# Sums of squares of x read from V's buffers, and V's last weights split before q and k are finished

## The chip, the core and the metric

The kernel runs on one core of one Trainium2 chip. The core has TensorE (matrix products), VectorE (DVE), ScalarE (ACT), GpSimd (POOL) and SyncE (SP), which issues nearly all transfers here. The metric is the device time of one launch in microseconds (us); lower is better.

## The reference, cut to what matters

The layer takes 512 tokens of width 1024. Of it, this change touches the root mean square norm at the start and the projections behind it.

```python
def rmsnorm(x, g):
    xf = x.astype(jnp.float32)
    y = xf * lax.rsqrt(jnp.mean(xf * xf, axis=-1, keepdims=True) + RMS_EPS)
    return (y * g.astype(jnp.float32)).astype(x.dtype)
...
        h = rmsnorm(x, g_mix[i])
        proj = h @ w_in[i]
        q_sb, k_sb, v_sb, z_sb, q_mb, k_mb, v_mb, z_mb = jnp.split(proj, split_at, axis=-1)
```

Eight stick-breaking heads (sb) and eight block heads (mb, with a slope times the distance of key and query, and a causal mask) follow. Their normed and gated outputs go through w_out, are added to x, and a second gated projection of p is added after another norm. All is float32.

## The kernel before, in words

Every float32 product is made of three TensorE products: an operand is split into a high part (cast on ScalarE, `part_hi`) and a low part (the difference, on VectorE, `part_lo`), and `mul3` multiplies high by high, high by low and low by high. x comes in twice: transposed (`xT`, four loads into `xt`), to be scaled by the gains and split into `hT` (`hT_hi`, `hT_lo`, eight slices k); and by tokens (`xs`, four loads of 512 KB), whose only use is the sum of squares of each token (`sq_x`, on ScalarE, with an accumulator). The norm's factor r (`find_r`: one VectorE step, one power on GpSimd) is not applied to `hT` but to the results of the projections: as a column of four numbers to V, and spread over a whole tile (`spread_r`: four TensorE transposes, one ScalarE copy) to q and k.

Weights are loaded in units of 512 KB into three buffers (tag `raw`), in the order q0, k0, the four V units, q1, k1 and on. Here the V units are called Vu0 to Vu3. A unit is split by two casts and two differences of 128x512, which `split_unit` puts into a queue; each `pop_w` issues the next cast and the difference of the cast before. The second difference of a unit frees its raw buffer and issues the load of the unit three further on. So Vu1's load follows q0's split, Vu2's follows k0's, and Vu3's follows Vu0's.

TensorE works through an order written by hand: warming products, the products of p with w_ple (`ple`), q0 and k0 (24 products each), V for token tiles 0 and 1 (48 products; k = 0, 1 use Vu0; 2, 3 use Vu1; 4, 5 use Vu2; 6, 7 use Vu3), the scores of head 0, and then a stream in which heads and projections alternate to the end. The four transposes of `spread_r` stand between k0's step 6 and step 7. The scores of head 0 need `end_q0` and `end_k0`: each takes the projection out of its bank times r (`scaled`, one VectorE product into the single buffer `ev`), then casts and differences: for q four casts of 64x512 on ScalarE, two differences on VectorE, and two zero fills on GpSimd; for k two casts and two differences.

Inside the section `start` the instructions of ScalarE and VectorE keep the order in which the program writes them. SyncE and (before) GpSimd are ordered by the planner; so are the instructions of ScalarE and VectorE written after the section, and the planner can put those between the ones inside it. The buffers of tag A and C, used later by the heads, hold `xt` first and `xs` second, so that load t of x waits until `hT_lo` has read chunk t of `xt`. The tag v has two buffers of 8 KB a partition for V's two halves, unused until V is taken out. `pl_d` is a DRAM tile into which the eight results of `ple` are parked by 256 KB stores. `rel` is the table of distances with the mask; `front_mb` scales it on ScalarE before each block head, by 4 for the first and by 0.5 for each later one.

Of the kernel before, what the change touches and what calls it, by code (L numbers as in the profile page):

```python
# [8 lines left out]
F32 = mybir.dt.float32  # L9
F32R = mybir.dt.float32r  # L10
BF16 = mybir.dt.bfloat16
AF = mybir.ActivationFunctionType
OP = mybir.AluOpType
ET = mybir.EngineType

P = 128
S = 512
DM = 1024
KT = DM // P
HD = 64  # L20
NH = 8
NPAIR = 8
DPLE = 256
NT = S // P
EPS = 1e-6
QKS = 0.125
NEG = -1e30
# [7 lines left out]
def layer(ctx, tc, x, xT, pT, w_qkz, w_v, gcols, g_final, w_out, w_ple, w_gate, out):  # L35
# [12 lines left out]
    nc = tc.nc  # L48
# [7 lines left out]
    at = ctx.enter_context(tc.tile_pool(name="at", bufs=2))  # L56
    dram = ctx.enter_context(tc.tile_pool(name="dram", bufs=1, space=bass.MemoryType.DRAM))
    pp = ctx.enter_context(tc.tile_pool(name="pp", bufs=1, space=bass.MemoryType.PSUM))
    ctx.enter_context(tc.manual_schedule(engines={ET.PE}))
    start = tc.manual_schedule(engines={ET.Activation, ET.DVE})  # L60
    start.__enter__()

    pl_d = dram.tile([NT, P, DM], F32, name="pl_d")
# [16 lines left out]
    def part_hi(hi, src, scale=None):  # L80
        if scale is None:
            nc.scalar.copy(hi, src)  # L82
        else:
            nc.scalar.activation(hi, src, AF.Copy, scale=scale)

    def part_lo(hi, lo, src, scale=None):
        if scale is None:
            nc.vector.tensor_sub(lo, src, hi.bitcast(F32))  # L88
        else:
            nc.vector.scalar_tensor_tensor(lo, src, scale, hi.bitcast(F32), op0=OP.mult, op1=OP.subtract)  # L90
# [11 lines left out]
    fq, wq, late = deque(), deque(), []  # L102
    pend = []

    def pop_w():
        if wq:
            hi, lo = wq.popleft()
            hi()
            if pend:
                pend.pop(0)()  # L110
            pend.append(lo)
        elif pend:
            pend.pop(0)()
# [43 lines left out]
    def load(tile_, src):  # L157
        nc.sync.dma_start(tile_, src)  # L158

    def load_unit():  # L160
        if n_load[0] == len(UNITS):
            return
        kind, a, u = key = UNITS[n_load[0]]
        n_load[0] += 1
        r = raws[key] = raw.tile([P, DM], F32, name="raw")
        if kind == "v":
            load(r, w_v[a, u])
        elif kind == "V":
            load(r.rearrange("p (g c) -> p g c", g=2),
                 w_v[:2, u // 2, :, u % 2 * S:(u % 2 + 1) * S].rearrange("g p c -> p g c"))  # L170
        elif kind == "o":
            half, n = a
            row = (4 * half + 2 * u) * P
            load(r.rearrange("p (k c) -> p k c", k=2),
                 w_out[row:row + 2 * P, n * S:(n + 1) * S].rearrange("(k p) c -> p k c", p=P))
        elif kind == "g":
            load(r, w_gate[a * P:(a + 1) * P, :])
        else:
            load(r, w_qkz[12 * (a // 4) + BASE[kind] + a % 4])

    def gate_tiles(k):

        if k < 2:
            if k == 0:
                wg["big"] = big.tile([P, 2, 2, DM], F32R, name="wg01", tag="hTl")
            w = wg["big"][:, k]
        elif k == 2:
            w = at.tile([P, 2, DM], F32R, name="wg2", tag="v")
        elif k == 3:
            w = wu.tile([P, 2, DM], F32R, name="wg3", tag="wu")  # L190
        else:
            tags = {4: ("QH0", "QH1", "K0", "K1"), 5: ("QH0", "QH1", "K0", "K1"), 6: ("QL0", "QL1", "QL0", "QL1"),
                    7: ("y0", "y1", "y2", "y3")}[k]
            w = [(yp if g[0] == "y" else at).tile([P, S], F32R, name=f"wg{k}{i}", tag=g)
                 for i, g in enumerate(tags)]
            return [(w[n], w[2 + n]) for n in range(2)]
        return [(w[:, 0, n * S:(n + 1) * S], w[:, 1, n * S:(n + 1) * S]) for n in range(2)]

    def split_unit():

        if n_split[0] == len(UNITS):
            return
        kind, a, u = key = UNITS[n_split[0]]
        n_split[0] += 1
        parts = []
        scale = gc[:, 2 * KT + a:2 * KT + a + 1] if kind == "g" else None

        def hi_(n):
            if not parts:
                if kind == "g":  # L210
                    wg[a] = gate_tiles(a)
                    parts.extend(wg[a])
                else:
                    w = W_[key] = wu.tile([P, 2, DM], F32R, name="wu")
                    parts.extend((w[:, 0, n * S:(n + 1) * S], w[:, 1, n * S:(n + 1) * S]) for n in range(2))
            part_hi(parts[n][0], raws[key][:, n * S:(n + 1) * S], scale)

        def lo_(n):
            part_lo(*parts[n], raws[key][:, n * S:(n + 1) * S], scale)
            if n:  # L220
                whole.add(key)
                load_unit()

        wq.extend((lambda n=n: hi_(n), lambda n=n: lo_(n)) for n in range(2))
        if n_split[0] < len(UNITS) and UNITS[n_split[0]][0] == "g":
            split_unit()
# [37 lines left out]
    load_unit()  # L264
    load_xt(3)
    load_unit()
    xs = [at.tile([P, DM], F32, name=f"xs{t}", tag="A" if t < 2 else "C") for t in range(NT)]

    def load_xs(t):
        load(xs[t], x[t * P:(t + 1) * P, :])  # L270

    for t in range(NT):
        load_xs(t)
# [10 lines left out]
    own = cst.tile([P, S], F32, name="own")  # L284
    nc.gpsimd.memset(own, 0.0)
    nc.gpsimd.affine_select(out=own, in_=own, compare_op=OP.not_equal, fill=1.0, base=S - P,
                            pattern=[[-1, S]], channel_multiplier=1)
    rel = at.tile([P, S], F32, name="rel", bufs=1)
    nc.gpsimd.iota(rel, pattern=[[1, S]], base=-384, channel_multiplier=-1,
                   allow_small_or_imprecise_dtypes=True)  # L290
    nc.gpsimd.affine_select(out=rel, in_=rel, compare_op=OP.is_ge, fill=NEG, base=384,
                            pattern=[[-1, S]], channel_multiplier=1)


# [209 lines left out]
    ss4, r4 = (cst.tile([P, NT], F32, name=n) for n in ("ss4", "r4"))  # L504

    def sq_x(t):
        junk = at.tile([P, DM], BF16, name="junk", tag="o")
        nc.scalar.activation(junk, xs[t], AF.Square, accum_out=ss4[:, t:t + 1])

    def find_r():  # L510

# [57 lines left out]
    for t in range(NT):  # L569
        sq_x(t)  # L570
# [6 lines left out]
    spread_r()  # L577
    F0(1)
    end_q0, end_k0 = first
    end_q0()  # L580
    split_unit()
    for _ in range(3):
        pop_w()
    end_k0()
    for t in range(NT):
        for n in range(2):
            load(pl_d[t, :, n * S:(n + 1) * S], pls[t, n])
    F0(8)
    pop_w()
    pop_w()  # L590

    start.__exit__(None, None, None)


    def scores(h):
        pr, e = divmod(h, 2)
        (Qh, Ql), k_ = Q[pr], K[pr][e]
        sc = pp.tile([P, 3 * S], F32, name="sc")
        for i in (3, 2, 0, 1):
            n = P * (i + 1)  # L600
            o = sc[:, OFF[i]:OFF[i] + n]
            q = slice(i * P, (i + 1) * P)
            mm(o, Qh[e][:, q], k_[:, :n], True, False)
            mm(o, Ql[e][:, q], k_[:, :n], False, True)
        return sc

    def rows(i):
        return OFF[i], OFF[i] + P * (i + 1)
# [34 lines left out]
        ])  # L643

    def front_mb(h):
        nc.scalar.activation(rel, rel, AF.Copy, scale=0.5 if h > NH else 0.5 / QKS)
        sc = scores(h)
        s = at.tile([P, WID], F32, name="A")
        w = W[h] = at.tile([P, WID], F32, name="C")
        m, nm, l, rl = (sm.tile([P, NT], F32, name=n) for n in ("m", "nm", "l", "rl"))  # L650

        def top(i):
            a, b = rows(i)
            nc.vector.tensor_tensor_reduce(out=s[:, a:b], in0=sc[:, a:b], in1=rel[:, S - (b - a):], scale=1.0,
                                           scalar=-3e38, op0=OP.add, op1=OP.max, accum_out=m[:, i:i + 1])

        def neg(c):
            nc.vector.tensor_scalar_mul(nm[:, c], m[:, c], -QKS)  # L658

        def exp(i):  # L660
            a, b = rows(i)
            nc.scalar.activation(w[:, a:b], s[:, a:b], AF.Exp, scale=QKS, bias=nm[:, i:i + 1],  # L662
                                 accum_out=l[:, i:i + 1])

        def inv(c):
            nc.vector.reciprocal(rl[:, c], l[:, c])

        def norm(i):
            a, b = rows(i)
            nc.vector.tensor_scalar_mul(w[:, a:b], w[:, a:b], rl[:, i:i + 1])  # L670

        hi, lo = slice(2, 4), slice(0, 2)
        fq.extend([
            lambda: top(3),
            lambda: (top(2), neg(hi)),
            lambda: (exp(3), exp(2), top(0), top(1), neg(lo)),
            lambda: (exp(0), exp(1)),
            lambda: (inv(hi), norm(3), norm(2)),
            lambda: (inv(lo), norm(0), norm(1)),
        ])  # L680
# [249 lines left out]
    t = NT - 1  # L930
# [75 lines left out]
```

## Time and profile before

| | us |
|---|---|
| median of 3 runs | 358.45 |
| lowest and highest | 357.63, 358.76 |
| the profiled execution, device time | 358.52 |
| its span, first to last instruction | 356.7 |
| TensorE busy | 345.5 (97%) |
| VectorE busy | 274.1 (77%) |
| ScalarE busy | 222.8 (62%) |
| GpSimd busy | 20.1 (6%) |

The device time of the profiled execution is 1.8 us above its span. The granted TensorE clock was 0.995 of full speed over the span. A busy share of TensorE counts pipelined products, whose recorded durations overlap; the distance from one start to the next is what a product costs.

### The profile page before, as it was taken

The page shows a single profiled execution, that of the slowest core. Times are in us where ns is not written, and L with a number is a line of the kernel's source. Part 1 is how long each engine was busy: PE and PEld are TensorE (multiplying, and loading weights), DVE is VectorE, ACT ScalarE, POOL GpSimd, SP SyncE. Part 2 cuts the span into 40 slices and gives each one's busy share as a digit, 9 for nine tenths or more (in the row PEclk, how much of TensorE's full clock was granted, in tenths as well). Part 3 has the DMA queues.
Part 4 walks back from the last instruction along what each step waited for, and adds up shares of the span by engine and source line. Part 5 has one row for each costly group of instructions (what it writes and reads, how often), then busy time and mean ns, then how long its engine had stood idle before and what let it go on. Part 6 is the DMA issues. An engine that isn't in the chain of part 4 may idle for free.

```text
span 356.7 us, 5077 instructions
## 1 busy us (share of the span) xinstructions
PE 345.5 (97%) x1808; PEld 292.1 (82%) x1808; DVE 274.1 (77%) x560; ACT 222.8 (62%) x421; POOL 20.1 (6%) x43
## 2 busy tenths in 40 slices
PE   8998899999999999999999999999999999999991
PEld 6786788888888888899888899888888888888891
DVE  4746779979898987988789888889799987244454
ACT  4887567664867464775596787598676662343341
POOL 6001000000000000000000100000000010010011
PEclk9999999999999999999999999999999999999998
DMA  6988907111131113112311302311811650022221
GB/s 214 379 291 272 311 9 232 62 61 59 59 119 60 59 62 130 56 64 104 122 59 61 118 3 59 119 59 30 326 59 63 212 200 0 7 100 71 90 89 59
DMA packets 14953, 40.18 MB, mean 113 GB/s; under 512 B 1616, under 2 KB 1872, under 8 KB 14928
## 3 DMA queue, kind: packets, MB, share of 16 engines
q1 hardware_dynamic: 14784, 39.60, 32.5%
q8 instruction: 14, 0.23, 0.3%
q10 hardware_dynamic: 144, 0.26, 0.2%
q14 instruction: 11, 0.09, 0.1%
HBM read 35.66 MB, written 4.19 MB: 112 GB/s over the span
## 4 chain that ended last, share of the span: by engine, by line
PE 84%; DMA 6%; issue 3%; DVE 2%; SPq 2%; ACT 1%; POOL 0%; POOLq 0%; ACTq 0%; DVEq 0%
PE pj L70 62%; PE sc L70 8%; PE tp L73 6%; PE av L70 6%; DMA raw<-in_w_qkz_dram 4%; DMA raw<-in_w_v_dram 2%; SPq L158 2%; PE tp L70 1%; DVE wu L88 1%; ACT wu L82 1%; DVE hTl L90 0%; DVE K L330 0%; POOL r L99 0%; POOLq L1002 0%; DVE ot L927 0%
## 5 line engine op out<-in xcount | busy, mean ns | idle before, releaser
L70 PE MATMUL pj<-hTh,wu 128*128 128x512 f32 x384 | 133.7, 400 | 0.0
L70 PEld LDWEIGHTS pj<-hTh,wu 128*128 128x128 f32 x384 | 72.2, 188 | 13.5 <-DVE wu L88 0.4
L70 PE MATMUL pj<-hTl,wu 128*128 128x512 f32 x192 | 75.1, 391 | 0.0
L82 ACT CAST wu<-raw 128x512 fp32r<-128x512 f32 x80 | 46.6, 617 | 23.1 <-PE pj L70 21.3
L88 DVE TENSOR_TENSOR wu<-raw,wu 128x512 fp32r<-128x512 f32 x80 | 52.7, 684 | 3.8 <-ACT wu L82 3.4
L70 PE MATMUL pj<-wg,h 128*128 128x512 f32 (+1 forms) x216 | 46.2, 371 | 0.0
L70 PEld LDWEIGHTS pj<-wg,h 128*128 128x128 f32 x216 | 36.9, 188 | 6.9
L70 PEld LDWEIGHTS pj<-hTl,wu 128*128 128x128 f32 x192 | 36.2, 189 | 5.2
L70 PE MATMUL pj<-wu,hTh 128*128 128x256 f32 (+1 forms) x160 | 34.2, 308 | 0.0
L82 ACT CAST ph<-tp 128x512 fp32r<-128x512 f32 (+1 forms) x48 | 24.5, 511 | 14.7 <-PE tp L73 14.4
L88 DVE TENSOR_TENSOR plo<-tp,ph 128x512 fp32r<-128x512 f32 (+1 forms) x48 | 28.5, 594 | 4.6 <-ACT ph L82 4.4
L70 PE MATMUL pj<-wu,yh 128*128 128x512 f32 x96 | 30.9, 402 | 0.0
L626 DVE TENSOR_TENSOR_SCAN inc<-A,own 128x512 f32<-128x512 f32 (+3 forms) x32 | 24.6, 809 | 5.6 <-ACT A L621 5.5
L70 PEld LDWEIGHTS pj<-wu,hTh 128*128 128x128 f32 x160 | 25.8, 191 | 1.3
L73 PE MATMUL tp<-idf,C 128*128 128x128 f32 x160 | 25.2, 272 | 0.0
L73 PEld LDWEIGHTS tp<-idf,C 128*128 128x128 f32 x160 | 20.3, 140 | 5.6
L70 PE MATMUL pj<-wu,hTl 128*128 128x256 f32 (+1 forms) x80 | 24.3, 304 | 0.0
L305 DVE TENSOR_TENSOR ev<-pj,rx 128x512 f32<-128x512 f32 x24 | 16.5, 686 | 6.3 <-PE pj L70 6.1
L70 PE MATMUL sc<-K,QH 128*128 128x512 f32 (+1 forms) x64 | 19.8, 322 | 0.0
L70 PE MATMUL av<-ph,v 128*128 128x512 f32 (+1 forms) x64 | 19.7, 309 | 0.0
L662 ACT ACTIVATE C<-A,nm 128x512 f32<-128x512 f32 (+3 forms) x32 | 17.8, 557 | 2.4 <-DVE nm L658 2.3
L70 PE MATMUL av<-plo,v 128*128 128x512 f32 (+1 forms) x64 | 19.1, 324 | 0.0
(135 smaller groups left out, 565.5 us busy)
## 6 DMA issues: line engine op xcount, KB each, us to landing
raw<-in_w_qkz_dram SPq DMA_DIRECT2D x24, 512.0 KB, 3.6
raw<-in_w_v_dram SPq DMA_DIRECT2D x8, 512.0 KB, 3.6
raw<-in_w_out_dram SPq DMA_DIRECT2D x8, 512.0 KB, 4.0
raw<-in_w_gate_dram SPq DMA_DIRECT2D x8, 512.0 KB, 3.6
xt<-in_xT_dram SPq DMA_DIRECT2D x4, 512.0 KB, 8.4
xs<-in_x_dram SPq DMA_DIRECT2D x4, 512.0 KB, 4.9
pl_d<-pt SPq DMA_DIRECT2D x8, 256.0 KB, 5.7
x<-in_x_dram SPq DMA_DIRECT2D x4, 512.0 KB, 6.5
```

The source lines that it names most:

```text
L70: nc.tensor.matmul(ps, lhsT=lhsT, rhs=rhs, start=start, stop=stop)
L73: nc.tensor.transpose(ps, src, idf)
L82: nc.scalar.copy(hi, src)
L88: nc.vector.tensor_sub(lo, src, hi.bitcast(F32))
L158: nc.sync.dma_start(tile_, src)
L305: nc.vector.tensor_mul(t, ps, rx["all"])
L626: nc.vector.tensor_tensor_scan(inc[:, c:c + b - a][:, ::-1], keep[:, a:b][:, ::-1], own[:, S - (b - a):][:, ::-1], 0.0, op0=OP.mult, op1=O ...
L662: nc.scalar.activation(w[:, a:b], s[:, a:b], AF.Exp, scale=QKS, bias=nm[:, i:i + 1], accum_out=l[:, i:i + 1])
```

## The change

Four edits. x by tokens is loaded into two tiles with V's tag, two token tiles each; token tiles 0 and 2 are squared on ScalarE as before, 1 and 3 on VectorE in place, with an accumulator. Behind `spread_r` the order on ScalarE and VectorE is: three pops (Vu2, and the first cast of Vu3), `end_q0`, the rest of Vu3, `end_k0`, and q1 only after that; before it was `end_q0`, three pops, `end_k0`, with the rest of Vu3 behind. GpSimd too keeps program order in the section, and `rel` is built at the section's end rather than at the kernel's start. `rel` is built with the factor 4 in it, so that the first block head scales nothing.

```diff
-    start = tc.manual_schedule(engines={ET.Activation, ET.DVE})
+    start = tc.manual_schedule(engines={ET.Activation, ET.DVE, ET.Pool})
...
-    xs = [at.tile([P, DM], F32, name=f"xs{t}", tag="A" if t < 2 else "C") for t in range(NT)]
+    xs = [at.tile([P, 2, DM], F32, name=f"xs{t}", tag="v") for t in range(2)]
...
-        load(xs[t], x[t * P:(t + 1) * P, :])
+        load(xs[t // 2][:, t % 2], x[t * P:(t + 1) * P, :])
...
-    rel = at.tile([P, S], F32, name="rel", bufs=1)
-    nc.gpsimd.iota(rel, pattern=[[1, S]], base=-384, channel_multiplier=-1,
-                   allow_small_or_imprecise_dtypes=True)
-    nc.gpsimd.affine_select(out=rel, in_=rel, compare_op=OP.is_ge, fill=NEG, base=384,
-                            pattern=[[-1, S]], channel_multiplier=1)
...
-        junk = at.tile([P, DM], BF16, name="junk", tag="o")
-        nc.scalar.activation(junk, xs[t], AF.Square, accum_out=ss4[:, t:t + 1])
+        x_ = xs[t // 2][:, t % 2]
+        if t % 2:
+            nc.vector.tensor_tensor_reduce(out=x_, in0=x_, in1=x_, scale=1.0, scalar=0.0, op0=OP.mult, op1=OP.add,
+                                           accum_out=ss4[:, t:t + 1])
+        else:
+            junk = at.tile([P, DM], BF16, name="junk", tag="o")
+            nc.scalar.activation(junk, x_, AF.Square, accum_out=ss4[:, t:t + 1])
...
     end_q0, end_k0 = first
-    end_q0()
-    split_unit()
     for _ in range(3):
         pop_w()
+    end_q0()
+    while wq or pend:
+        pop_w()
     end_k0()
+    split_unit()
     for t in range(NT):
         for n in range(2):
             load(pl_d[t, :, n * S:(n + 1) * S], pls[t, n])
...
+    rel = at.tile([P, S], F32, name="rel", bufs=1)
+    step = int(0.5 / QKS)
+    nc.gpsimd.iota(rel, pattern=[[step, S]], base=-384 * step, channel_multiplier=-step,
+                   allow_small_or_imprecise_dtypes=True)
+    nc.gpsimd.affine_select(out=rel, in_=rel, compare_op=OP.is_ge, fill=NEG, base=384,
+                            pattern=[[-1, S]], channel_multiplier=1)
     start.__exit__(None, None, None)
...
-        nc.scalar.activation(rel, rel, AF.Copy, scale=0.5 if h > NH else 0.5 / QKS)
+        if h > NH:
+            nc.scalar.activation(rel, rel, AF.Copy, scale=0.5)
```

## Rows read from the trace of the kernel before

**Rows 1.** The page: 40 slices of 8.9 us, TensorE's busy tenths and transfer rate.

```profile
PE   8998899999999999999999999999999999999991
...
GB/s 214 379 291 272 311 9 232 62 61 59 59 119 60 59 62 130 56 64 104 122 59 61 118 3 59 119 59 30 326 59 63 212 200 0 7 100 71 90 89 59
```

**Rows 2.** Waits of TensorE, 16 to 44 us: total, times, longest (us).

```profile
PE av L70 <- DVE wu L88: 1.4, 2, 1.1
PE tp L73 <- POOL r L99: 0.7, 1, 0.7
```

**Rows 3.** Timeline of TensorE: start, duration, instruction, count, idle before and releaser.

```profile
26.68 0.39 PE L70 MATMUL pj<-hTh,wu 128*128 128x512 f32 x1
27.73 0.65 PE L73 MATMUL tp<-idf,r 128*128 128x128 f32 x4 [0.67 <-POOL r L99]
...
34.13 0.39 PE L70 MATMUL tp<-wu,hTl 128*128 128x512 f32 x1
...
34.84 0.50 PE L70 MATMUL av<-wu,hTh 128*128 128x512 f32 x1 [0.32 <-ACT wu L82]
...
35.65 0.50 PE L70 MATMUL av<-wu,hTh 128*128 128x512 f32 x1 [0.31 <-DVE wu L88]
...
38.26 0.43 PE L70 MATMUL av<-wu,hTh 128*128 128x512 f32 x1
...
39.78 0.50 PE L70 MATMUL av<-wu,hTh 128*128 128x512 f32 x1 [1.09 <-DVE wu L88]
...
42.41 0.39 PE L70 MATMUL sc<-K,QH 128*128 128x512 f32 x1
```

**Rows 4.** Timeline of ScalarE, VectorE and GpSimd, 15 to 40 us.

```profile
15.05 0.62 ACT L646 ACTIVATE rel<-rel 128x512 f32<-128x512 f32 x1
...
20.70 1.06 ACT L508 ACTIVATE junk<-xs 128x1024 bf16<-128x1024 f32 x1
...
21.16 1.28 DVE L88 TENSOR_TENSOR wu<-raw,wu 128x512 fp32r<-128x512 f32 x2
...
26.39 0.17 DVE L98 TENSOR_SCALAR rs_t<-ss 128x4 f32<-128x4 f32 x1 [3.94 <-ACT junk L508]
...
26.65 1.03 POOL L99 TENSOR_TENSOR r<-rs_t,mhalf 128x4 f32<-128x4 f32 x1 [20.31 <-DVE rs_t L98]
27.15 1.29 DVE L88 TENSOR_TENSOR wu<-raw,wu 128x512 fp32r<-128x512 f32 x2 [0.59 <-ACT wu L82]
...
36.23 1.27 ACT L329 CAST K<-ev 64x512 fp32r<-64x512 f32 x2
...
36.99 1.40 DVE L330 TENSOR_TENSOR K<-ev,K 64x512 fp32r<-64x512 f32 x2
...
38.43 1.89 DVE L88 TENSOR_TENSOR wu<-raw,wu 128x512 fp32r<-128x512 f32 x3
```

**Rows 5.** Timeline of SyncE's issues, 5 to 29 us.

```profile
5.89 0.58 SPq L158 DMA_DIRECT2D raw<-in_w_qkz_dram  x1
...
7.26 0.96 SPq L158 DMA_DIRECT2D raw<-in_w_qkz_dram  x1
14.39 6.61 SPq L158 DMA_DIRECT2D xs<-in_x_dram  x4
21.05 1.79 SPq L158 DMA_DIRECT2D raw<-in_w_v_dram  x3
...
28.48 0.37 SPq L158 DMA_DIRECT2D raw<-in_w_v_dram  x1
```

**Rows 6.** Issue to landing by tile: raw (6 to 9 us), raw (22 to 30).

```profile
DMA to landing us min/median/max: 9.6/10.1/10.7
...
DMA to landing us min/median/max: 3.6/5.4/7.2
```

**Rows 7.** VectorE by form: reduction of two inputs; busy us, mean ns, idle before.

```profile
L654 DVE CUSTOM_DVE_ANT_0 A<-sc,rel 128x512 f32<-128x512 f32 x8 | 5.5, 683 | 0.6 <-PE sc L70 0.6
...
L654 DVE CUSTOM_DVE_ANT_0 A<-sc,rel 128x128 f32<-128x128 f32 x8 | 2.3, 283 | 0.0
```

## Prediction

> **What bounds the kernel now.** I read the 40 slices first. TensorE is at nine tenths or more in all slices but a few at the start and the last one [rows 1], so only time in which TensorE is kept waiting can be won. The view of waits says where that is: between 16 and 44 us TensorE waits for differences of weights on VectorE and for r from GpSimd [rows 2], and from 44 to 338 us it lists no wait of TensorE longer than its threshold. So the case is decided before 44 us, and what TensorE gains there should reach the end unchanged.
>
> The waits view counts idle time after the modelled end of a product; what a stall costs is the distance between starts above the usual pitch. From the timeline of TensorE the pitch in a row of 512-column products is 0.227 us (in this stretch, three in 0.68). Against it the four gaps are [rows 3]:
>
> - the transposes of `spread_r`: 27.73 - 26.68 - 0.23 = 0.82, waiting for r;
> - Vu2's casts: 34.84 - 34.13 - 0.23 = 0.48;
> - Vu2's last difference: 35.65 - 34.84 - 0.23 = 0.58;
> - Vu3's differences: 39.78 - 38.26 - 0.23 = 1.29.
>
> The sum is 3.17 us, 0.9% of the span. It is the ceiling of this change in the stretch it edits.
>
> Next, what was late. r starts from the fourth sum of squares; the step on VectorE began at 26.39 and the power ran from 26.65 to 27.68 [rows 4]. The four loads of x were issued between 14.39 and 21.00, although SyncE had been done with its first batch at 8.2 [rows 5]: each waited for `hT_lo` to release its buffer. The V units stand behind x in SyncE's order, so they too were only issued from 21.05. And Vu3's differences came at 38.43, after the casts of K (36.23) and its differences (36.99 to 38.39), which stand ahead of them in program order [rows 4]. So the last and largest stall is one of order: K's 1.40 us of VectorE work, not needed before the scores at 42.41, went ahead of weights for which TensorE already stood waiting since 38.5.
>
> **x in V's buffers.** The buffers of tag v are free until V is taken out, so x is issued right behind k0's load, at about 8.5, and queues. How fast does the queue drain? q0 was issued at 5.89 and landed 9.6 later (15.5), k0 at 7.26 and landed 10.7 later (17.95) [rows 5, 6], with one load of the same size between: two loads in 2.45, or 1.23 us per 512 KB. In order of issue that gives x at 19.2, 20.4, 21.6, 22.9; Vu0 at 24.1; Vu1, released by q0's split, at 25.3; Vu2, released by k0's split at 22.44, at 26.6 (before: 22.5 + 7.2 = 29.7 [rows 6]).
>
> **Squares on two engines.** ScalarE squares tile 0 at 20.70 as before, and tile 2 behind it, done by about 22.9. VectorE's reduction of two inputs of 1024 columns is not in the trace; the nearest rows are 683 ns for 512 and 283 ns for 128 columns [rows 7], so 1.04 ns per column and 1.22 us for 1024. Bounds are ScalarE's 1.06 for the same tile [rows 4] and twice the 512-column row, 1.37; I take 1.22, the line through the two rows. VectorE is free at 22.44, so tile 1 ends at 23.7 and tile 3 at 24.9. The step for r ends at 25.2, the power, 0.26 behind its start and 1.03 long [rows 4], at about 26.3. TensorE comes to the transposes at 26.91. So r is 0.6 us early (0.3 with 1.37 per square), and the first stall, 0.82, goes.
>
> **V's last units first.** ScalarE: transposes done 27.6, copy of r to 28.2, Vu2's casts to 29.4 (0.6 each), where before they began only at 33.6 behind four casts of Q. Vu2's differences end at 30.1; TensorE wants them at about 34.0. The 0.48 and the 0.58 go. Vu0's differences follow the step for r, 25.2 to 26.5, and then Vu3's load is issued; it lands 3.6 later as before [rows 6], at 30.1. Its first cast ends at 30.7. Q is queued behind that cast on ScalarE: four casts of 0.64 to 33.3, then Vu3's second cast to 33.9, Vu3's last difference to 34.6 on VectorE. TensorE wants Vu3 at 38.26 less the three stalls gone, 36.4. The 1.29 goes with 1.8 us to spare.
>
> K comes last: from `ev` (0.69) to 35.3, then, as before from first cast to last difference (36.23 to 38.39), 2.16: done at 37.5. The scores want it at 42.41 - 3.17 = 39.2, so K has 1.7 us to spare. This is the one new dependence: everything behind Vu3's first cast waits for Vu3's landing, and K ends 7.4 us after it. Landing up to 31.8 costs nothing; each us later costs one us.
>
> **GpSimd in program order.** Power, then two zero fills for Q, then `rel`, then the fills of `inc`. All are wanted after 39 us (`rel` only at the first block head, past 170 us), and GpSimd does nothing else before 39: no cost. Moving `rel` from the start takes nothing off TensorE, whose first product waits for another fill.
>
> Here a rule speaks against the change. The row: beside the power, which reads SBUF until 27.68, two differences started at 27.15 and took 1.29 together; a pair with GpSimd quiet took 1.28 [rows 4]. So GpSimd's work delays VectorE by nothing here. The Trainium skill, "SBUF — State Buffer", section "SBUF: two separate sides", says that a VectorE instruction with two SBUF inputs and a GpSimd one that reads SBUF exclude each other for a whole instruction. By that, the first difference would have begun at 27.68, which the trace contradicts. By the rule Vu0's differences here would wait 1.1 for the power, and K's another 1.0 for the filling of `rel` if that holds the port as long: 2.1 against 1.7 to spare, 0.4 more on the sum. I go by the row.
>
> **One scaling less, and q1.** The first scaling of `rel` had been put at 15.05, 0.62 on ScalarE [rows 4], just before q0's first cast at 15.57. q0 landed at 15.5, so taking it out moves that cast by 0.1 at most; I count nothing. q1's split moves behind K; TensorE wants q1 past 50 us.
>
> **The sum.** 358.52, the profiled execution's own time, less 3.17 is 355.35. I add 0.25 for hand-overs between engines that I have taken as tight, since r's margin is only 0.6: 355.6. The profiled time is 0.07 above the median of the runs shown, which changes nothing. What a measurement can tell from no change is 0.3%, or 1.1 us; the forecast is 0.8% faster.
>
> **The rivals.**
>
> *The wait moves to Vu3 and K.* SyncE's order is the planner's, and the eight 256 KB stores to `pl_d` are ready early. If several enter the queue ahead of Vu3, it lands late. The slices at 27 to 45 us show 272 to 311 GB/s [rows 1], 0.84 to 0.96 us per store. Six ahead after Vu2's 26.6 give 26.6 + 5.4 + 1.2 = 33.2, 1.4 past the free limit: 357.0. All eight give 35.0 and hand back all 3.2: 358.5. For it: in the stalled stretch the transfers ran at about that rate, so the queue was in use. Against it: in program order the stores come after `end_k0`, later than Vu3's load, and before the change Vu3 landed in 3.6.
>
> *Only r is won.* If V's weights come no earlier, because casts and transfers and not their order hold them, the 0.82 alone goes: 357.7, no measurable change. Against it: ScalarE idled for x, and Vu2 lay landed for 3.9 us (29.7 to 33.6) before its cast.
>
> *Slower: the loads share and don't queue.* If x, put into the queue at 8.5, takes its part of the transfer rate while xt's last chunk and k0 are under way, k0 comes later than 17.95. Its first cast stands on ScalarE ahead of the last two slices of `hT`, which had about 0.6 us to spare; each us beyond that stops TensorE in q0. It passes the 3.2 gained when k0 lands 3.8 late, at 21.8. Were all five loads of k0 and x to end together at 22.9, k0 would be 4.9 late and the stall 4.3: 355.4 + 4.3 = 359.7. Against it: q0 and k0 landed 2.45 apart with many loads outstanding, in order [rows 5, 6]. The Trainium skill, "DMA: Bandwidth & Descriptors", section "Queues, rings and completion order", says that descriptors are consumed in ring order but completion need not follow the order of issue; by its first half k0 keeps its 17.95, by its second some of this rival could come true, and the two landings bear out the first.
>
> **How the numbers follow.** All stalls gone: 0.72, 355.6, own range 354.9 to 356.3. The wait moved to Vu3 and K: 0.14, 356.3 to 358.5, two thirds of it below 357.4. Only r: 0.07, 357.7. Slower: 0.07, 359.7. Faster by over 0.3% (below 357.4): 0.72 + 0.09 = 0.81. Within 0.3%: 0.05 + 0.07 = 0.12. Slower 0.07. The range goes from the ceiling with a little beyond it, 354.8, to 357.6, which takes in most of the second case and leaves out nearly all of the last two.
>
> **What would show it.** x landing by 23 and squares on VectorE between 22.4 and 25; the power ending before 26.9; no gap of TensorE above 0.3 us between 16 and the scores; Vu2's casts near 28, Vu3 landing near 30, K's last difference near 37.5; the first score product near 39.2 rather than 42.41, and from there on every row of TensorE earlier by the same 3 us to the end. I am wrong if the stores stand ahead of Vu3, if k0 lands after 18.5, if a square on VectorE takes much over 1.4, or if the planner, which orders the rest anew, opens a wait of TensorE past 44 us where there is none.

## The result and the profile after

The changed kernel takes 354.79 us (median of 6, 354.69 to 356.66) against 359.13 for the kernel before in the same runs. The ratio is 0.9889, 95% interval 0.9857 to 0.992: 1.1% faster. A second measurement (below) gave 0.9905, 0.9886 to 0.9924. The forecast was 355.6 with a range of 354.8 to 357.6, so the median lies at the lower end. The forecast took 2.9 us off the time before; the two ratios stand for 4.0 and 3.4 us.

The page's slices of TensorE, which answer to [rows 1]:

```profile
PE   8999999999999999999999999999999999999991
```

Only the first and the last slice are left below nine tenths. The view of TensorE's waits from 16 to 44 us, which answers to [rows 2], has no row any more. The timeline of TensorE, which answers to [rows 3]:

```profile
26.57 0.39 PE L70 MATMUL pj<-hTh,wu 128*128 128x512 f32 x1
26.79 0.60 PE L73 MATMUL tp<-idf,r 128*128 128x128 f32 x4
...
27.93 0.39 PE L70 MATMUL av<-wu,hTh 128*128 128x512 f32 x1
...
36.10 0.62 PE L70 MATMUL av<-wu,hTh 128*128 128x512 f32 x2
...
38.59 0.40 PE L70 MATMUL tp<-wu,hTl 128*128 128x512 f32 x1
38.83 0.39 PE L70 MATMUL sc<-K,QH 128*128 128x512 f32 x1
```

The transposes follow the product before them at the pitch of 0.23, and the scores start at 38.83 instead of 42.41: 3.58 us earlier. That gain arrives at the end unchanged. The last row of the chain (the work that ended last, followed back) is the same instruction in both traces; first before, then after:

```profile
352.40 0.72 ACT ot L969
```

```profile
348.82 0.72 ACT ot L979
```

From the scores to that row it is 352.40 - 42.41 = 309.99 before and 348.82 - 38.83 = 309.99 after. What happens behind the scores takes as long in both profiles, to 0.01 us, so the case lies wholly ahead of them.

Why nothing waits there now, in the timeline after (ScalarE, VectorE, GpSimd and SyncE, which answer to [rows 4, 5]):

```profile
27.91 1.14 ACT L82 CAST wu<-raw 128x512 fp32r<-128x512 f32 x2
29.25 0.62 ACT L82 CAST wu<-raw 128x512 fp32r<-128x512 f32 x1 [0.19 <-DMA raw<-in_w_v_dram]
...
21.38 1.22 DVE L504 CUSTOM_DVE_ANT_0 xs<-xs 128x1024 f32<-128x1024 f32 x1
...
23.86 0.17 DVE L98 TENSOR_SCALAR rs_t<-ss 128x4 f32<-128x4 f32 x1
24.34 2.61 DVE L88 TENSOR_TENSOR wu<-raw,wu 128x512 fp32r<-128x512 f32 x4 [0.31 <-ACT wu L82]
...
33.14 1.29 DVE L88 TENSOR_TENSOR wu<-raw,wu 128x512 fp32r<-128x512 f32 x2
...
35.72 1.41 DVE L325 TENSOR_TENSOR K<-ev,K 64x512 fp32r<-64x512 f32 x2 [0.69 <-ACT K L324]
...
24.12 1.03 POOL L99 TENSOR_TENSOR r<-rs_t,mhalf 128x4 f32<-128x4 f32 x1 [21.38 <-DVE rs_t L98]
...
8.23 4.04 SPq L158 DMA_DIRECT2D xs<-in_x_dram  x4
13.20 8.66 SPq L158 DMA_DIRECT2D raw<-in_w_v_dram  x3
...
25.66 0.37 SPq L158 DMA_DIRECT2D raw<-in_w_v_dram  x1
```

x is issued from 8.23 without a wait for `hT_lo`. r is ready at 24.12 + 1.03 = 25.15, 1.6 us ahead of the transposes. Vu2's casts start at 27.91; in the timeline of ScalarE before, they are in this row:

```profile
33.64 1.66 ACT L82 CAST wu<-raw 128x512 fp32r<-128x512 f32 x3
```

Vu3's differences (33.14 to 34.43) now stand ahead of K's (35.72 to 37.13), and TensorE wants them at 36.1 and 38.8.

### The profile page after: what moved, and what is told of

Its sections match the earlier page's. It is cut to its first block, busy times and chain, and to the rows that moved or that the text cites. A ratio compares the mean times of both kernels' runs of the same rounds, so it can differ in the third digit from the quotient of the medians.

```text
span 353.1 us, 5079 instructions
## 1 busy us (share of the span) xinstructions
PE 344.2 (97%) x1808; PEld 292.4 (83%) x1808; DVE 276.1 (78%) x564; ACT 220.3 (62%) x416; POOL 19.6 (6%) x43
## 4 chain that ended last, share of the span: by engine, by line
PE 93%; issue 3%; DMA 1%; DVE 1%; ACT 1%; POOL 0%; POOLq 0%; SPq 0%; DVEq 0%; ACTq 0%
PE pj L70 67%; PE sc L70 9%; PE av L70 8%; PE tp L73 6%; PE tp L70 3%; DMA rawh<-in_pT_dram 1%; POOL r L99 0%; POOLq L1012 0%; SPq L158 0%; DVE ot L937 0%; ACT ot L979 0%; DVE x L908 0%; DVE tmp L905 0%; ACT tmp L904 0%; DVE pu L88 0%
## 5 line engine op out<-in xcount | busy, mean ns | idle before, releaser
L82 ACT CAST ph<-tp 128x512 fp32r<-128x512 f32 (+1 forms) x48 | 24.5, 511 | 14.7 <-PE tp L73 14.5
```

## The experiments

Times vary from one execution of the same kernel to the next (the kernel before took 356.98 to 360.34 beside the first four of these runs), so I read each run twice: its ratio, and in its profile the stage from the transposes to the first score product. The last column is that stage; all but the ratios are in us.

| kernel | ratio to before (95%) | transposes | scores | between |
|---|---|---|---|---|
| before | | 27.73 | 42.41 | 14.68 |
| before, second profile | | 27.55 | 42.33 | 14.78 |
| rel alone | 0.9995 (0.9975, 1.0015) | 26.48 | 41.28 | 14.80 |
| x and squares alone | 0.9951 (0.9929, 0.9973) | 26.56 | 39.86 | 13.30 |
| order alone | 0.9935 (0.9912, 0.9959) | 26.93 | 38.97 | 12.04 |
| order alone, second profile | | 27.15 | 39.52 | 12.37 |
| changed | 0.9889 (0.9857, 0.992) | 26.79 | 38.83 | 12.04 |
| changed, again | 0.9905 (0.9886, 0.9924) | 26.85 | 38.88 | 12.03 |
| changed, squares on ScalarE | 0.991 (0.988, 0.994) | 28.58 | 40.62 | 12.04 |
| changed, stores first | 0.9979 (0.9956, 1.0003) | 27.52 | 41.70 | 14.18 |
| changed, x ahead of k0 | 1.0063 (1.003, 1.0096) | 31.91 | 44.20 | 12.29 |
| changed, start filled | 0.9905 (0.9887, 0.9924) | 27.28 | 39.31 | 12.03 |

**x and squares alone.** The diff's edits of `xs`, `load_xs` and `sq_x`, on the kernel before.

```diff
+    xs = [at.tile([P, 2, DM], F32, name=f"xs{t}", tag="v") for t in range(2)]
...
+        if t % 2:
+            nc.vector.tensor_tensor_reduce(out=x_, in0=x_, in1=x_, ...
```

> Only x in V's buffers and the shared squares; order of the splits and GpSimd as before. By the theory of the forecast (early x cures the wait for r; the order cures the wait for Vu3): r is ready before the transposes, that gap (0.82 us) is gone; Q's casts start near 28.7 and Vu2's near 31.3, whose differences end at 33.2, just in time; Vu3's differences still stand behind K's and end near 37.3 where TensorE wants them at 36.2, so a gap of about 1.1 us stays there. Gain over the kernel before 2.5 us (2.0 to 2.8). Rival, that earlier transfers alone do all of it: no gap left, gain 3.4 us or more. Rival, that x is worth only the wait for r: gain 0.8 us.

Measured 0.9951, 1.7 us faster (by the interval 1.0 to 2.5), less than the 2.5 expected; between the two profiles the scores start 42.41 - 39.86 = 2.55 earlier. The timeline of its TensorE has one gap left in V:

```profile
35.87 0.39 PE L70 MATMUL av<-wu,hTh 128*128 128x512 f32 x1
37.20 0.50 PE L70 MATMUL av<-wu,hTh 128*128 128x512 f32 x1 [0.94 <-DVE wu L88]
```

37.20 - 35.87 - 0.23 = 1.10 us, before Vu3's differences, where and as large as the expectation said. Vu2's two gaps are gone without any change of order, as it said too. In the timeline of ScalarE:

```profile
28.53 0.62 ACT L320 CAST QH<-ev 64x512 fp32r<-64x512 f32 x1 [0.76 <-DVE ev L305]
...
31.10 1.66 ACT L82 CAST wu<-raw 128x512 fp32r<-128x512 f32 x3
```

Vu2's casts still stand behind Q's, but all of them start 2.5 us earlier (31.10 against 33.64), since r and the first V units are there earlier. So early x is neither all of the gain nor worth the wait for r alone.

**Order alone.** The diff's edit around `end_q0` and `end_k0`, on the kernel before.

```diff
-    end_q0()
-    split_unit()
     for _ in range(3):
         pop_w()
+    end_q0()
+    while wq or pend:
+        pop_w()
     end_k0()
+    split_unit()
```

> Only the order: Vu2 and Vu3 split ahead of q's and k's ends; x, squares and GpSimd as before. By the theory of the forecast the 0.82 us wait for r stays; Vu2's casts run from 30.1, Vu3 lands at 32.05 as before, its last difference is done near 36.5 and K near 39.4, both just ahead of need, so the three gaps in V (0.48, 0.58, 1.29) and the restarts behind them go: gain 2.4 to 2.7 us. Rival, that without early x Vu3 lands too late for this order and the wait moves to Vu3 and K: a gap of 0.5 us or more ahead of the scores, gain under 2 us.

In the profile all three gaps in V are gone, 14.7 to 12.04, as in the whole change; the time fell by 2.3 us (1.5 to 3.2). The wait for r that the expectation kept is not there: the transposes follow at the pitch.

```profile
26.71 0.39 PE L70 MATMUL pj<-hTh,wu 128*128 128x512 f32 x1
26.93 0.60 PE L73 MATMUL tp<-idf,r 128*128 128x128 f32 x4
```

A second profile of two kernels followed that up.

> A second look at the kernel with only the order changed, whose profiled execution took 355.05 and whose other executions mostly 356.8 to 357.2. By the theory that late x costs a varying wait for r: a gap of 0.5 to 1.9 us stands at the transposes here if the execution is one of the longer ones, and none if it is a short one. Rival, that the difference lies ahead of q0 (a clock that rises later): q0 starts past 17.5 and no gap stands at the transposes.

> A second look at the kernel before, unchanged. By the theory of a varying wait for r: the gap at the transposes differs from the 0.82 of the first profile (it may be nothing), while the gaps at Vu2's and Vu3's weights, which come of the order, sum to 2.3 us again within 0.4.

The order alone again had no gap at the transposes (27.15 after 26.93); its V stage took 12.37. It took 355.82, so it was no example of the executions at 356.8 to 357.2 (six of nine), and what makes those longer stays open. The kernel before, profiled again (358.41), shows the varying wait (TensorE, then VectorE's step for r):

```profile
27.32 0.39 PE L70 MATMUL pj<-hTh,wu 128*128 128x512 f32 x1
27.55 0.60 PE L73 MATMUL tp<-idf,r 128*128 128x128 f32 x4
...
35.12 0.50 PE L70 MATMUL av<-wu,hTh 128*128 128x512 f32 x1 [0.31 <-DVE wu L88]
...
38.02 0.51 PE L70 MATMUL av<-wu,hTh 128*128 128x512 f32 x1
39.70 0.50 PE L70 MATMUL av<-wu,hTh 128*128 128x512 f32 x1 [1.17 <-DVE wu L88]
...
25.90 0.17 DVE L98 TENSOR_SCALAR rs_t<-ss 128x4 f32<-128x4 f32 x1 [3.82 <-ACT junk L508]
```

No wait for r here: TensorE itself came 0.64 later (q0 started at 17.35, in the first profile at 16.39), and the step for r started at 25.90 rather than 26.39. The gaps of the order are there again, 39.70 - 38.02 - 0.23 = 1.45 the largest. So the wait for r is a race of two paths that end within 1 us of each other, and the gaps of the order come every time: the stage took 14.68, 14.78 and, with rel alone, 14.80.

**rel alone.** GpSimd in program order, `rel` late with its factor, one scaling less, on the kernel before.

> Only GpSimd in program order, the table of distances built late with its factor in it, one scaling less. By the theory of the forecast: nothing, within 0.3 us. Rival, that the scaling taken off ScalarE at 15.05 lets q0 start with fewer waits: up to 0.3 us faster, q0's products from first to last in 10.0 rather than 10.3 us. Rival, the shared port of GpSimd and VectorE: differences that run beside the table's fill take over 1 us, 0.4 us slower.

0.9995: nothing, as forecast. Neither rival came: two differences beside the table's fill took 1.29, as elsewhere, and the short 10.0 us of q0's and k0's products up to the transposes stands in the second profile of the kernel before too, with the scaling still in it.

**Squares on ScalarE.** The changed kernel with the four squares where they were.

```diff
-        if t % 2:
-            nc.vector.tensor_tensor_reduce(out=x_, in0=x_, in1=x_, ...
-        else:
-            junk = at.tile([P, DM], BF16, name="junk", tag="o")
-            nc.scalar.activation(junk, x_, AF.Square, accum_out=ss4[:, t:t + 1])
+        junk = at.tile([P, DM], BF16, name="junk", tag="o")
+        nc.scalar.activation(junk, x_, AF.Square, accum_out=ss4[:, t:t + 1])
```

> The changed kernel with all four squares on ScalarE. By the theory of the forecast sharing is not what wins: x lands by 22.3, four squares of 1.05 us from 19.7 end at 24.0, the step for r starts near 24.2 rather than 23.86, and the power still ends ahead of the transposes at 26.8: same time as the changed kernel within 0.3 us (3.4 to 3.9 us faster than before in the profile). Rival, that r is tight and sharing buys part of the gain: the transposes wait 0.3 us or more.

0.991, no difference from the change that its interval can show. The first square and r's step and power; the first row is the changed kernel's, the others this run's:

```profile
19.71 1.05 ACT L508 ACTIVATE junk<-xs 128x1024 bf16<-128x1024 f32 x1
...
21.13 1.06 ACT L504 ACTIVATE junk<-xs 128x1024 bf16<-128x1024 f32 x1
...
25.43 0.17 DVE L98 TENSOR_SCALAR rs_t<-ss 128x4 f32<-128x4 f32 x1 [2.56 <-ACT junk L504]
...
25.69 1.03 POOL L99 TENSOR_TENSOR r<-rs_t,mhalf 128x4 f32<-128x4 f32 x1 [22.95 <-DVE rs_t L98]
```

r is ready at 26.72, 1.6 us later than with shared squares, but sharing makes little of that: ScalarE came to the first square 1.42 later in this execution, and from there to the step for r it took 25.43 - 21.13 = 4.30 against 23.86 - 19.71 = 4.15. TensorE came to the transposes 1.8 later as well, at 28.58, for a reason told below, so r was 1.9 early and nothing waited. That sharing the squares buys anything is not shown.

**Stores first.** The changed kernel with SyncE in program order too, and the eight stores ahead of the sums of squares.

```diff
-    start = tc.manual_schedule(engines={ET.Activation, ET.DVE, ET.Pool})
+    start = tc.manual_schedule(engines={ET.Activation, ET.DVE, ET.Pool, ET.SP})
...
+    for t in range(NT):
+        for n in range(2):
+            load(pl_d[t, :, n * S:(n + 1) * S], pls[t, n])
     for t in range(NT):
         sq_x(t)
     find_r()
```

> The changed kernel with SyncE too in program order in the section and the eight stores to pl_d written ahead of the sums of squares, so that all eight enter the queue between Vu2's load and Vu3's. This makes the rival of the forecast (the wait moves to Vu3 and K) true on purpose. By the forecast's rule (K ends 7.4 us after Vu3 lands, and each us past the free limit costs one): in the changed kernel stores land 0.65 us apart, so Vu3 lands near 32.5 rather than 29.2, K ends near 40 rather than 37.1, TensorE loses 0.9 to 1.6 us ahead of k = 6 and of the scores, and the time is that much above the changed kernel's 354.8. By the forecast's own price for eight stores (0.9 us each, landing at 35.0) it would lose 3.2. Rival, that stores and loads overlap and cost nothing: Vu3 lands by 30.5, no gap.

Timeline of its SyncE, ScalarE, VectorE and TensorE:

```profile
22.27 5.55 SPq L158 DMA_DIRECT2D pl_d<-pt  x8
27.91 0.58 SPq L158 DMA_DIRECT2D raw<-in_w_v_dram  x1
...
34.51 0.62 ACT L82 CAST wu<-raw 128x512 fp32r<-128x512 f32 x1 [4.73 <-DMA raw<-in_w_v_dram]
...
40.26 1.41 DVE L325 TENSOR_TENSOR K<-ev,K 64x512 fp32r<-64x512 f32 x2 [0.69 <-ACT K L324]
...
38.25 0.49 PE L70 MATMUL av<-wu,hTh 128*128 128x512 f32 x1 [1.26 <-ACT wu L82]
39.03 0.50 PE L70 MATMUL av<-wu,hTh 128*128 128x512 f32 x1 [0.28 <-DVE wu L88]
...
41.70 0.40 PE L70 MATMUL sc<-K,QH 128*128 128x512 f32 x1
...
62.79 0.44 PE L70 MATMUL av<-plo,v 128*128 128x384 f32 x1 [0.17 <-DVE plo L88]
...
298.99 0.66 PE L73 MATMUL tp<-idf,x 128*128 128x128 f32 x4 [0.36 <-DVE x L435]
```

Vu3 landed just before 34.51, later than I expected for this run and close to the forecast's 35.0. K ended at 40.26 + 1.41 = 41.67, 7.2 us behind it (forecast 7.4), and the scores started that moment. The stage took 14.18 instead of 12.03, a loss of 2.15: more than the 0.9 to 1.6 that I expected for this run, less than the forecast's 3.2. Vu3 landed 0.5 earlier than the forecast's price had it, and TensorE came to the transposes 0.6 later than the forecast had it (27.52 against 26.91), which gives K as much more room; 2.15 + 0.5 + 0.6 is that price again. In the profiled execution, one of the longer ones at 358.87 (median 357.63), a further 1.1 us went behind the scores: half of it at 62.79, where TensorE waited for a difference on VectorE, half at 298.99, where it waited for a residual sum there. Waits past 44 us are the last of the dangers that the forecast named; that they come of the planner's order is not shown. The ratio, 0.9979, gives back 2.6 to 3.2 us of the 3.4 to 4.0.

**x ahead of k0.** The changed kernel with one `load_unit()` moved behind x's loads.

> The changed kernel with the four loads of x issued ahead of k0's, which makes k0 five us late on purpose. If loads land in the order of issue, x lands 1.2 us earlier than in the changed kernel and k0 at 21.8 rather than 16.9; k0's cast then holds back the last two slices of hT on ScalarE and TensorE stops in q0 near step 6 for 3 to 3.5 us; the time is 357.5 to 358.5, close to the kernel before. If loads share the rate, k0 moves by under 3 us and TensorE stops for under 2 us.

Timeline of its ScalarE and TensorE:

```profile
23.28 0.62 ACT L82 CAST wu<-raw 128x512 fp32r<-128x512 f32 x1 [4.88 <-DMA raw<-in_w_qkz_dram]
23.81 1.33 ACT L84 ACTIVATE hTh<-xt,gc 128x512 fp32r<-128x512 f32 x2
...
22.14 0.39 PE L70 MATMUL pj<-hTh,wu 128*128 128x512 f32 x1
24.57 0.51 PE L70 MATMUL pj<-hTh,wu 128*128 128x512 f32 x1 [2.04 <-ACT hTh L84]
25.36 0.50 PE L70 MATMUL pj<-hTl,wu 128*128 128x512 f32 x1 [0.28 <-DVE hTl L90]
```

k0, issued at 12.05 and landed 11.2 later, came at 23.3, more than the 21.8 expected. The four loads of x ahead of it landed 1.2 to 1.3 apart (17.0 to 20.8) and k0 behind them all, so loads behind one another queue and don't share; why k0 came 2.4 behind the last of them and not 1.2 is not shown. TensorE stopped for 24.57 - 22.14 - 0.23 = 2.20 and 0.56 more, and r (its sums wait for k0's split) for another 0.2. The whole from q0 to the transposes took 13.6 us against 10.2. q0 also started 1.7 later in this execution (18.29 against 16.59), which I read as hidden: had it started earlier, TensorE would have stopped longer for k0. The time is 361.07, 1.0063 of before and 2.6 above the 358.5 at which my expectation ended. k0 was 6.3 later than in the changed kernel and the transposes 5.1; the forecast's rule (all of k0's delay beyond 0.6) gives 5.7. So the forecast's slower rival, forced, does end on that side.

**Start filled, and the change again.** In `ple`, seven products of the zero tile, into a bank not yet used, where TensorE idled at 5 to 6.5 us.

```diff
+                if (k, t, n) == (0, 1, 0):
+                    fill(4)
                 mm(pls[t, n], hi, wp[n][:, k, 0, :], k == 0, False)
+                if (k, t, n) == (0, 1, 0):
+                    fill(3)
```

> The changed kernel, unchanged, again, beside the next kernel. By the theory of what is known now (the order is worth 2.6 us, early x 0 to 0.8 at the transposes, and single executions are 1.9 us longer when TensorE's full clock is granted near 10 us rather than near 5): most executions at 354.6 to 355.2, some near 356.7; faster than the kernel before by 3 to 4 us.

> The changed kernel with seven more warming products of 128 columns put where TensorE idles between 5 and 6.5 us in the products of p (four ahead of the second token tile, three behind its first product); they compute nothing that is used. Theory: the full clock comes late in those executions in which TensorE idled there, so with the holes filled all executions stand at 354.6 to 355.2, none near 356.7; the lowest time stays that of the changed kernel within 0.3 us. Rival: the late clock has nothing to do with these holes, and executions near 356.7 remain as often as in the changed kernel. Rival: the fillers push the real products back by 0.3 us or more in all executions.

Both 0.9905; 354.71 to 355.58 and 354.80 to 355.39. Neither had an execution near 356.7, so the filler could not show whether it removes them. In its profile q0 started at 17.08 against 16.65, but its median is 0.05 us from the change's: it is no version that beats the change.

## Why the prediction was right, step by step

- **Only waits ahead of 44 us count, and what is gained there reaches the end.** Shown: 309.99 us from the scores to the chain's end in both profiles.
- **x queues behind k0 and the V units move up.** The fixed step per load held: x landed 9.9 to 10.4 after issue, at 18.1, 19.5, 20.7 and 22.3 (forecast 19.2, 20.4, 21.6, 22.9), and "x ahead of k0" showed the order of landing. Vu3 was issued at 25.66 and cast at 29.25, 0.9 earlier than forecast.
- **Squares.** 1.22 us each on VectorE, the figure taken from the two rows of [rows 7].
- **r.** Ready at 25.15, forecast 26.3. The step whose size was wrong is here: "the first stall, 0.82, goes" counted a wait of one execution as the kernel's. Of five profiles with x loaded late in its old buffers (before twice, rel alone, order alone twice) one has it. It is also the one in which the first weights landed latest: q0 at 15.5 and k0 at 17.95, in the other four at 14.4 to 15.1 and 16.9 to 17.6. k0's first cast stands ahead of the last slices of `hT`, and the last load of x waits for those, so a late k0 makes r late. In the changed kernel k0 landed at 17.0, 0.97 ahead of the forecast's 17.95, and r came 1.15 ahead of its forecast. Early x makes r safe (0.9 to 2.0 us early in the six profiles that have it in V's buffers behind k0), and what that is worth varied from 0 to 0.8 in the profiles.
- **The order of Vu3 and K.** "The 1.29 goes with 1.8 us to spare", shown both ways: with x alone 1.10 stays, with the order alone nothing stays. K's last difference at 37.13 (forecast 37.5), scores at 38.83 (39.2).
- **Vu2's 0.48 and 0.58** go with either part alone. The prediction gave them to the order only. So in the stage from transposes to scores the parts overlap: x alone wins 1.4, the order 2.6, both 2.6.
- **GpSimd, rel and one scaling less: nothing.** 0.9995. In the changed kernel the power ran from 24.12 to 25.15 beside differences that took 0.65 each. The Trainium skill's rule that the prediction names ("SBUF — State Buffer", section "SBUF: two separate sides") would have held them until 25.15. The row contradicts it once more, as far as GpSimd's spans tell, which the profile gives only roughly.
- **The reserve of 0.25** was not needed. The change won 3.58 between these two profiles against 3.17 less 0.25. The stage from transposes to scores gave 14.68 - 12.04 = 2.64, where the gaps had counted 2.35: restarting the stream of products after the gaps costs some 0.3 more than the gaps. (The products behind those at 35.65 and 39.78 [rows 3] start at 35.98 and 40.12, 0.33 and 0.34 later, where the pitch is 0.23.) The transposes came 0.94 earlier: r's 0.82, another 0.31 between q0's first product and the transposes (10.29 us from 16.39 to 26.68 before, 9.98 from 16.59 to 26.57 after), less 0.20 because q0 started later. I claim neither for the change: in the second profile of the kernel before, and with rel alone and x alone, the stretch of 10.29 takes 9.97, and q0's start moves from run to run.
- **Rivals.** The wait did not move to Vu3 and K, because one store and not eight stood ahead of Vu3; forced, it cost 2.15 in that stage against a price of 3.2, for the reasons above. That only r is won is out: the order alone wins 2.6 behind r. The slower rival did not come, since loads queue.
- **Luck.** That the forecast of the time came near is in part luck: it counted 0.82 that four of five such profiles don't have, and left out the 0.3 of the restarts and whatever makes the change better than the order alone.

What stays open: two ratios of the change, 3.4 and 4.0 us, are above the 2.6 that the order wins in the profiles and the 2.3 that it wins in time. x alone won 1.7 in time, so by whole executions the two parts nearly add, which the overlap in the stage does not explain. Six of nine executions of "order alone" took 356.8 to 357.2, eleven of twelve of the change 354.7 to 355.6. The rest may be a mixture of r's race and of how q0 starts; that is not shown, since the executions of "order alone" near 357 were not caught in a profile.

## What to carry to other kernels

Where an in-order engine splits weights and also finishes results, issue what the bottleneck needs next ahead of what it needs later; here 1.4 us of K's work that had 4 us to spare stood ahead of weights for which TensorE was waiting. Move loads with no true dependence to buffers that are free, but behind the loads that are needed sooner: the same four loads put in front of k0 made the kernel 6 us slower than the change. And take a second profile before a wait is counted: one that comes of two paths ending within 1 us is a race, and its size in one trace is not its price.

## What the runs showed of the hardware that I had not expected

TensorE's first products sometimes run at half speed for longer. In "squares on ScalarE", with the start of the program as in the changed kernel, the timeline of TensorE shows:

```profile
5.92 1.81 PE L70 MATMUL pj<-wp,pu 128*128 128x512 f32 x3 [0.32 <-ACT pu L82]
7.54 2.76 PE L70 MATMUL tp<-wp,pu 128*128 128x512 f32 x6
10.10 1.64 PE L70 MATMUL pj<-wp,pu 128*128 128x512 f32 x6
```

and the changed kernel:

```profile
5.87 1.32 PE L70 MATMUL pj<-wp,pu 128*128 128x512 f32 x3 [0.37 <-ACT pu L82]
7.03 1.55 PE L70 MATMUL tp<-wp,pu 128*128 128x512 f32 x6
```

The six products from 7.54 take (10.10 - 7.54) / 6 = 0.43 us each from start to start; in the changed kernel it is 0.23. At 1.2 GHz, the lower of TensorE's two clock levels, 512 cycles last 0.43, one for each column. The clock column reads 1.00 over this stretch in both, so the pitch is all that speaks for the lower level. In both, the warming products had run from 0.99 to 4.16 and TensorE idled briefly before 5.9. At 10.10 the first trace goes over to the short pitch. q0 then started at 18.38 instead of 16.59, and that execution took 356.70. Of the other ten profiles one, "x ahead of k0", shows the same (q0 at 18.29). One execution of the changed kernel in six took 356.66, 1.9 us above the others; that this was the same thing is a guess.
